# Four writes and one read for a turned tile, and a DRAM tile ordered by diagonal blocks

## The chip, the cores and the metric

The kernel runs on one core of one Trainium2 chip. The metric is the device time of one execution in microseconds (us), of which the median of several runs is taken. Before the change it is 2255.21 us (three runs, 2254.8 to 2257.08).

## The reference

One inference step of a two-layer hybrid recurrent decoder, for a prompt of 1024 tokens and for eight samples of one token each with states of their own, with the same float32 weights. The even layer has eight gated DeltaNet heads (GDN) beside eight mLSTM heads, the odd layer four GLA heads beside four retention heads:

```python
h = rms(x, norm_w) * (1.0 + scale) + shift
proj = h @ w_in                               # one projection per layer, 1024 -> several thousand columns
# GDN, per chunk of tokens:
A = where(tri_strict, decay * kk, 0.0) * beta
U = triangular_solve(A + eye, rhs, lower, unit_diagonal)
o = gam * (q @ S) + (qk * decay) @ U
S_new = exp(last) * S + k^T @ (exp(last - bh) * U)
# both branches:
y = concat(branch outputs) * silu(z)
x = x + gate * (y @ w_out)
```

What matters here is the triangular solve of GDN, and that keys and values are wanted both with channels and with tokens in the partitions, so that tiles have to be turned.

## The kernel before

All activations are kept with channels in the 128 partitions and 1032 columns (1024 prompt tokens, then eight samples). Prompt tokens are worked in eight chunks of 128. A projection to 128 channels is 72 matmuls of 344 columns into the three pj banks, with each weight tile split into a high and a low part (whi, wlo).

Nothing is issued in the order in which the Python stands. A `Recorder` takes down every operation with what it depends on (`add`, line 207, and `touch`, line 244), and `order` (line 274) plans all engines' queues with estimated durations: a list scheduler that runs forward, then backward for new priorities, up to ten times, and keeps the plan with the shortest estimated end. `emit` then issues the operations in that order, so that in the profile each carries the same line, 448. All DMAs go through one queue, SP. Each engine takes its instructions strictly in the planned order and waits at an instruction whose inputs aren't there, whatever stands behind it. The planner counts two accesses of a DRAM tile as dependent when their ranges from first to last element overlap (`region`, line 198), also where the elements themselves are interleaved and never the same. The built program's waits come from the tile framework and not from that rule.

Two helpers are touched by the change.

`squares` (line 1697) turns a tile: VectorE (DVE) transposes its 32 x 32 blocks into y, then the blocks are moved between partitions through a DRAM tile td (one of four, line 2145), and come back as z. Before, that is one DMA that writes y whole (512 KB) and four DMAs that read 32 partitions each (128 KB each). In one execution it is called 52 times. In the even layer there are 36: the keys and the values of each GDN head (written from s_kd and s_vs, by `gdn_mix`, line 1191), values and outputs of each mLSTM head (from s_va) and keys of each mLSTM pair (from s_kwe). In the odd layer there are 16, in `v_tokens` (line 1711). Tiles read back are named after the slot that they land in: s_N, s_v, s_mp, s_pt, s_qs, s_u.

`inverse` (line 1279), once for each GDN head, inverts eight 128 x 128 unit triangular matrices N. Their 32 x 32 diagonal blocks, four to a matrix (index j), are written to a DRAM tile nd by four DMAs of 32 KB, read back in one as 64 blocks of 16 x 16 in 64 partitions (into s_EM), inverted there in 15 steps of two DVE operations, written to a DRAM tile yd and read back by four DMAs. Small matmuls then build the whole inverse. (The tile yd of the inverse shares its name in the profile with the big tile yd that holds the mixer's output.) Before, rows of nd and yd are ordered by chunk c first, then j, then half q: the four writes interleave, and each one's range overlaps the next one's.

The 128 x 1024 tiles of weights are loaded into two slots wf0 and wf1, whose loads (wf<-in_ev_w_in, wf<-in_ada_w) wait for PE or DVE to free the slot, and stand in SP's queue among all else.

Of the kernel before, what the change touches and what calls it, by code (L numbers as in the profile page):

```python
# [9 lines left out]
F32 = mybir.dt.float32  # L10
# [7 lines left out]
T = 1024  # L18
# [6 lines left out]
NC = T // L  # L25
# [438 lines left out]
class Step:  # L464
# [814 lines left out]
    def inverse(self, N):  # L1279

        V, G, dma = self.nc.vector, self.nc.gpsimd, self.nc.sync.dma_start

        nd, yd = (self.nyd[x][self.turn(x, 2)] for x in ("nd", "yd"))
        by32 = lambda x, j: x.rearrange("(c j q) x -> c j (q x)", c=NC, j=4)[:, j, 0:1024].rearrange(
            "c (s t) -> s c t", t=32)
        by16 = lambda x: x[:, 0:512].rearrange("m (r t) -> m r t", t=32)[:, :, 0:16]
        blocks = [slice(32 * j, 32 * j + 32) for j in range(4)]
        t = self.slot("EM", name="inv")
        D, At, qt, Dt = (t[:, 256 * i:256 * i + 256].rearrange("p (c t) -> p c t", c=NC) for i in range(4))
        nb, yb, tb = (t[0:64, 256 * i:256 * i + 256].rearrange("p (r t) -> p r t", t=16) for i in (1, 2, 3))  # L1290
        dma(yb, self.a["i16"].rearrange("p (r t) -> p r t", t=16))
        for j, b in enumerate(blocks):
            dma(by32(nd, j), N[b, :, b])
        dma(nb, by16(nd))
        for s in range(15):
            n = 15 - s
            V.tensor_tensor(tb[:, 0:s + 1, 0:n], yb[:, 0:s + 1, s:s + 1].to_broadcast([64, s + 1, n]),
                            nb[:, s:s + 1, s + 1:16].to_broadcast([64, s + 1, n]), op=ALU.mult)
            V.tensor_tensor(yb[:, 0:s + 1, s + 1:16], yb[:, 0:s + 1, s + 1:16], tb[:, 0:s + 1, 0:n], op=ALU.subtract)
        dma(by16(yd), yb)  # L1300

        for j, b in enumerate(blocks):
            dma(D[b], by32(yd, j))
        V.transpose(Dt, D)
        p = self.ps(None, [128, NC, 32])
        for c in range(NC):
            for j, b in enumerate(blocks):
                self.mm(p[b, c, :], N[b, c, b], Dt[b, c, :], tile_position=(32 * j, 32 * j))
        V.tensor_tensor(At, p, self.imask.unsqueeze(1).to_broadcast([128, NC, 32]), op=ALU.mult)
        p = self.ps(None, [128, NC, 32])  # L1310
        for c in range(NC):
            for j, b in enumerate(blocks):
                self.mm(p[b, c, :], At[b, c, :], D[b, c, :], tile_position=(32 * j, 32 * j))
        V.tensor_tensor(D, D, p, op=ALU.subtract)
        V.transpose(Dt, D)
        Y = self.slot("Y", [128, NC, L], name="Y")
        G.memset(Y, 0.0)
        for b in blocks:
            V.tensor_copy(Y[b, :, b], D[b])

        p = self.ps(None, [128, 2, NC, 32])
        for c in range(NC):
            for i in (0, 2):
                j = i + 1
                bi, bj = slice(32 * i, 32 * i + 32), slice(32 * j, 32 * j + 32)
                self.mm(p[bj, 0, c, :], N[bi, c, bj], Dt[bi, c, :], tile_position=(32 * i, 32 * j))
        for j in (1, 3):
            bj = slice(32 * j, 32 * j + 32)
            self.act(qt[bj], p[bj, 0], AF.Copy, scale=-1.0)
        p2 = self.ps(None, [128, NC, 64])  # L1330
        for c in range(NC):
            for i in (0, 2):
                j = i + 1
                bi, bj = slice(32 * i, 32 * i + 32), slice(32 * j, 32 * j + 32)
                self.mm(p2[bi, c, 0:32], qt[bj, c, :], D[bj, c, :], tile_position=(32 * j, 32 * i))
            self.mm(p2[32:64, c, 0:32], D[32:64, c, :], qt[32:64, c, :], tile_position=(32, 32))
        V.tensor_copy(Y[0:32, :, 32:64], p2[0:32, :, 0:32])
        V.tensor_copy(Y[64:96, :, 96:128], p2[64:96, :, 0:32])

        iy = t[:, 0:512].rearrange("p (c t) -> p c t", c=NC)  # L1340
        Yt = iy[0:64]
        G.memset(Yt[0:32, :, 32:64], 0.0)
        G.tensor_copy(Yt[0:32, :, 0:32], Dt[0:32])
        G.tensor_copy(Yt[32:64, :, 32:64], Dt[32:64])
        V.tensor_copy(Yt[32:64, :, 0:32], p2[32:64, :, 0:32])
        p3 = self.ps(None, [128, NC, 64])
        for c in range(NC):
            self.mm(p3[64:128, c, :], N[0:64, c, 64:128], Yt[:, c, :], tile_position=(0, 64))
        q3 = iy
        self.act(q3[64:128], p3[64:128], AF.Copy, scale=-1.0)  # L1350
        p4 = self.ps(None, [128, NC, 64])
        for c in range(NC):
            self.mm(p4[0:64, c, :], q3[64:128, c, :], Y[64:128, c, 64:128], tile_position=(64, 0))
        V.tensor_copy(Y[0:64, :, 64:128], p4[0:64])
        return Y
# [341 lines left out]
    def squares(self, y, x, z):  # L1697


        dma = self.nc.sync.dma_start  # L1700
        y, z = y[:, 0:T], z[:, 0:T]
        self.nc.vector.transpose(y.rearrange("p (b c j) -> p b c j", b=4, c=NC),
                                 x[:, 0:T].rearrange("p (c b i) -> p b c i", b=4, c=NC))
        d = self.td[self.turn("td", 4)]
        dma(d, y)
        for b in range(4):
            dma(z[32 * b:32 * b + 32].rearrange("i (a x) -> i a x", a=4),
                d.rearrange("(a i) (b x) -> b i a x", a=4, b=4)[b])
        return z.rearrange("p (a c j) -> p c a j", a=4, c=NC)

    def v_tokens(self, v):
# [407 lines left out]
    def build(self):  # L2119
        tc, nc = self.tc, self.nc  # L2120
        with ExitStack() as ctx:
            cp = ctx.enter_context(tc.tile_pool(name="cp", bufs=1))
            psum = ctx.enter_context(tc.tile_pool(name="psum", bufs=1, space=PSUM))
            dr = ctx.enter_context(tc.tile_pool(name="dr", bufs=1, space=DRAM))
            self.big = {}
            for n in NAMES:
                for i in range(TAGS.get(n, 1)):
                    s = Slot(cp, f"s_{n}{i}", [128, SIZES.get(n, W)])
                    self.nc.slots[s.ap.name] = s
                    self.big[n, i] = s.ap  # L2130
            self.wt = {(n, i): cp.tile([128, 1024], F32 if n == "wf" else F32R, name=f"{n}{i}")
                       for n in WBUFS for i in range(WBUFS[n])}
            self.banks = {(n, i): psum.tile([128, 512], F32, name=f"{n}{i}")
                          for n in BANKS for i in range(BANKS[n])}
            self.arena = cp.tile([128, ARENA], F32, name="arena")
            self.base = cp.tile([128, BASE], F32, name="base")
            self.arena_at = {"base": 0, "even": 0, "odd": 0}
            self.xd = dr.tile([2, KT, 128, W], F32, name="xd")
            self.yd = dr.tile([16, 128, W], F32, name="yd")
            self.gd = dr.tile([4, 8, T], F32, name="gd")  # L2140
            self.ed = dr.tile([8, 8, 8], F32, name="ed")
            self.sd = [dr.tile([16, 128], F32, name=f"sd{i}") for i in range(2)]
            self.spd = dr.tile([16, W], F32, name="spd")
            self.rd = [dr.tile([4, QB], F32, name=f"rd{i}") for i in range(2)]
            self.td = [dr.tile([128, T], F32, name=f"td{i}") for i in range(4)]
            self.nyd = {x: [dr.tile([64, 528], F32, name=f"{x}{i}") for i in range(2)] for x in ("nd", "yd")}
            self.program()
            with tc.manual_schedule():
                self.nc.emit()
# [103 lines left out]
```

## Time and profile before

| what | value |
|---|---|
| median of three runs | 2255.21 us |
| profiled execution, its own time | 2262.98 us |
| its span, first to last instruction | 2261.2 us |
| mean granted TensorE clock | 0.983 |
| DMA traffic | 290.61 MB, mean 129 GB/s |

PE is TensorE's matmuls, PEld its weight loads, DVE VectorE, ACT ScalarE, POOL GpSimd, SP the queue that issues DMAs. A row of a stage gives the time span, then busy us and instruction count of each engine, the granted clock, the share of the DMA engines' time and GB/s. A row of waits gives an engine and the tile it writes, whom it waited for, us in total, times, longest. A row in order of time gives the start in us from the span's beginning, its us, engine, line, operation, output<-inputs, shapes and count; in brackets stands idle time just before and who ended it. On SP the time of a row is that of the issue, not of the transfer. The chain of work that ended last gives start, us and what.

### The profile page before, as it was taken

The page shows a single profiled execution, that of the slowest core. Times are in us where ns is not written, and L with a number is a line of the kernel's source. Part 1 is how long each engine was busy: PE and PEld are TensorE (multiplying, and loading weights), DVE is VectorE, ACT ScalarE, POOL GpSimd, SP SyncE. Part 2 cuts the span into 40 slices and gives each one's busy share as a digit, 9 for nine tenths or more (in the row PEclk, how much of TensorE's full clock was granted, in tenths as well). Part 3 has the DMA queues.
Part 4 walks back from the last instruction along what each step waited for, and adds up shares of the span by engine and source line. Part 5 has one row for each costly group of instructions (what it writes and reads, how often), then busy time and mean ns, then how long its engine had stood idle before and what let it go on. Part 6 is the DMA issues. An engine that isn't in the chain of part 4 may idle for free.

```text
span 2261.2 us, 42497 instructions
## 1 busy us (share of the span) xinstructions
PE 2184.1 (97%) x17532; PEld 2036.4 (90%) x17532; DVE 1312.8 (58%) x2559; ACT 761.4 (34%) x1374; POOL 588.4 (26%) x409
## 2 busy tenths in 40 slices
PE   6999999999999998998989999999999999999998
PEld 4877877999999988998889999999999999999997
DVE  6775656576565756666553355745754754755322
ACT  4432313242323323232341135234335334334322
POOL 3120212121121311202330032623622622634210
PEclk9999989999999999999999999999999999999999
DMA  9465564625172535527383222254253253365212
GB/s 263 134 190 161 138 190 115 177 78 149 48 189 75 160 99 123 137 77 189 100 253 117 74 80 69 73 153 124 76 157 119 76 162 106 110 192 176 81 59 92
DMA packets 323383, 290.61 MB, mean 129 GB/s; under 512 B 51963, under 2 KB 289013, under 8 KB 323182
## 3 DMA queue, kind: packets, MB, share of 16 engines
q1 hardware_dynamic: 323190, 287.91, 45.2%
q8 instruction: 137, 2.24, 0.4%
q14 instruction: 56, 0.46, 0.1%
HBM read 213.61 MB, written 74.44 MB: 127 GB/s over the span
## 4 chain that ended last, share of the span: by engine, by line
PE 81%; DMA 8%; DVE 6%; ACT 2%; issue 2%; SPq 1%; POOL 0%; POOLq 0%; ACTq 0%; DVEq 0%
PE pj L448 63%; PE A L448 12%; PE B L448 5%; SPq L448 1%; DMA wf<-in_ada_w 1%; DMA s_mp<-td 1%; DVE s_pt L448 1%; DVE wlo L448 1%; DMA s_h<-in_x_prompt 1%; DVE s_tmp L448 1%; DVE arena L448 1%; DMA td<-s_va 1%; DMA s_pt<-yd 0%; DMA td<-s_vs 0%; DMA s_pt<-td 0%
## 5 line engine op out<-in xcount | busy, mean ns | idle before, releaser
L448 PE MATMUL pj<-s_h,whi 128*128 128x344 f32 (+1 forms) x6024 | 1500.0, 328 | 3.7 <-DVE s_h L448 2.6
L448 PEld LDWEIGHTS pj<-s_h,whi 128*128 128x128 f32 (+1 forms) x6024 | 1046.5, 190 | 33.2 <-issue 19.8
L448 PE MATMUL pj<-s_h,wlo 128*128 128x344 f32 (+1 forms) x3024 | 985.2, 326 | 1.0 <-POOL s_h L448 0.6
L448 PEld LDWEIGHTS pj<-s_h,wlo 128*128 128x128 f32 (+1 forms) x3024 | 573.2, 190 | 12.1 <-issue 8.2
L448 ACT ACTIVATE whi<-wf 128x1024 fp32r<-128x1024 f32 (+1 forms) x146 | 152.1, 1042 | 355.1 <-PE pj L448 309.4
L448 DVE TENSOR_TENSOR wlo<-wf,whi 128x1024 fp32r<-128x1024 f32 x112 | 153.3, 1369 | 195.5 <-ACT whi L448 190.9
L448 ACT ACTIVATE s_pt<-pj 128x344 f32<-128x344 f32 (+1 forms) x170 | 76.7, 452 | 237.0 <-PE pj L448 232.4
L448 POOL TENSOR_TENSOR arena<-arena,base 128x8 f32<-128x8 f32 (+5 forms) x38 | 62.2, 1638 | 286.2 <-DVE arena L448 286.2
L448 POOL TENSOR_TENSOR wlo<-wf,whi 128x1024 fp32r<-128x1024 f32 (+1 forms) x32 | 77.4, 2419 | 169.0 <-ACT whi L448 163.5
L448 POOL TENSOR_TENSOR s_tmp<-s_EM 128x512 f32<-128x512 f32 (+1 forms) x60 | 81.3, 1368 | 81.7 <-DVE s_N L448 28.5
L448 DVE SCALAR_TENSOR_TENSOR s_pt<-s_u,base,s_pt 128x1024 f32<-128x1024 f32 x72 | 95.3, 1323 | 0.1
L448 ACT ACTIVATE s_u<-pj 128x344 f32<-128x344 f32 x93 | 41.2, 452 | 136.6 <-PE pj L448 86.8
L448 DVE SCALAR_TENSOR_TENSOR arena<-arena,A 128x128 f32<-128x128 f32 (+1 forms) x84 | 32.8, 390 | 92.5 <-PE A L448 92.4
L448 DVE SCALAR_TENSOR_TENSOR s_zz<-s_pt,pj 128x344 f32<-128x344 f32 x96 | 48.7, 507 | 62.8 <-ACT s_pt L448 62.1
L448 POOL TENSOR_TENSOR s_tmp<-s_tmp,arena 128x1024 f32<-128x1024 f32 (+2 forms) x26 | 45.3, 1747 | 83.2 <-PE B L448 34.2
L448 POOL MEMSET s_u<- 128x3 f32 x24 | 2.5, 102 | 243.4 <-DVE s_pt L448 243.4
L448 POOL TENSOR_TENSOR s_kd<-s_kd,s_vs 128x1032 f32<-128x1032 f32 x8 | 20.0, 2506 | 169.2 <-ACT s_vs L448 169.2
L448 ACT ACTIVATE s_tmp<-s_tmp 128x1024 f32<-128x1024 f32 (+1 forms) x44 | 46.1, 1057 | 35.7 <-POOL s_tmp L448 34.1
L448 DVE TENSOR_TENSOR s_EM<-s_EM 64x15 f32<-64x15 f32 (+7 forms) x240 | 49.9, 208 | 14.2 <-DMA s_EM<-nd 9.0
L448 DVE SCALAR_TENSOR_TENSOR arena<-arena,B 64x130 f32<-64x130 f32 (+1 forms) x84 | 31.2, 372 | 44.4 <-PE B L448 43.6
L448 ACT ACTIVATE arena<-A,arena 128x128 f32<-128x128 f32 x64 | 23.5, 367 | 92.9 <-PE A L448 92.7
L448 ACT ACT_TABLE_LOAD x41 | 52.6, 1283 | 5.1 <-DMA s_h<-in_x_prompt 4.3
(639 smaller groups left out, 3550.4 us busy)
## 6 DMA issues: line engine op xcount, KB each, us to landing
wf<-in_ev_w_in SPq DMA_DIRECT2D x64, 512.0 KB
wf<-in_od_w_in SPq DMA_DIRECT2D x48, 512.0 KB
wf<-in_ada_w SPq DMA_DIRECT2D x32, 512.0 KB
s_tmp<-sd SPq DMA_DIRECT2D x24, 512.0 KB
s_pt<-yd SPq DMA_DIRECT2D x16, 516.0 KB
td<-s_kd SPq DMA_DIRECT2D x16, 512.0 KB
td<-s_vs SPq DMA_DIRECT2D x16, 512.0 KB
s_v<-td SPq DMA_DIRECT2D x64, 128.0 KB
```

The costliest lines, as they stand in the source:

```text
L448: op.fn(*[self.placed(x) for x in op.args], **{k: self.placed(x) for k, x in op.kw.items()})
```

## The change

In `squares`, the write is cut into four DMAs, one for each 32 partitions a of y; each writes one quarter d[a] of the DRAM tile, whose shape becomes [4, 128, 256], in rows of 1 KB. One DMA reads the whole of it back into z. In `inverse`, rows of nd and yd are ordered by diagonal block j first, then chunk c, then half q, so that each of the four writes fills a range of its own. The 16 x 16 inversion works on whichever block lies in a partition, so nothing else changes with it.

```diff
-        by32 = lambda x, j: x.rearrange("(c j q) x -> c j (q x)", c=NC, j=4)[:, j, 0:1024].rearrange(
+        by32 = lambda x, j: x.rearrange("(j c q) x -> j c (q x)", c=NC, j=4)[j, :, 0:1024].rearrange(
             "c (s t) -> s c t", t=32)
...
         d = self.td[self.turn("td", 4)]
-        dma(d, y)
-        for b in range(4):
-            dma(z[32 * b:32 * b + 32].rearrange("i (a x) -> i a x", a=4),
-                d.rearrange("(a i) (b x) -> b i a x", a=4, b=4)[b])
+        for a in range(4):
+            dma(d[a].rearrange("(b i) x -> i b x", b=4), y[32 * a:32 * a + 32].rearrange("i (b x) -> i b x", b=4))
+        dma(z.rearrange("p (a x) -> p a x", a=4), d.rearrange("a p x -> p a x"))
...
-            self.td = [dr.tile([128, T], F32, name=f"td{i}") for i in range(4)]
+            self.td = [dr.tile([4, 128, 256], F32, name=f"td{i}") for i in range(4)]
```

Since the planner sees other dependencies and other sizes, it makes another order for the whole program. SP issues 990 DMAs before and after, and PE has the same matmuls.

On SP, at the inverse of the second GDN head, before (s_N0 is N, s_v20 the turned values of GDN, s_mp0 a turned mLSTM tile; in brackets the semaphores waited for, DMAHW those of DMAs):

```order
L448 DMA nd1_134<-s_N0_70 32x8x32 [waits DMAHW6_49]
L448 DMA wf1_105<-in_ev_w_in 128x8x128 [waits DMAHW7_49,PE_49]
L448 DMA s_v20_65<-td1_130 32x4x256 [waits DMAHW3_49,DMAHW0_49]
L448 DMA s_v20_65<-td1_130 32x4x256 [waits DMAHW1_49]
L448 DMA wf0_104<-in_ada_w 128x1024 [waits DMAHW2_49,DVE_49]
L448 DMA s_v20_65<-td1_130 32x4x256
L448 DMA s_v20_65<-td1_130 32x4x256 [waits DMAHW4_49]
L448 DMA nd1_134<-s_N0_70 32x8x32 [waits DMAHW5_49]
```

The same place now:

```order
L448 DMA nd1_134<-s_N0_70 32x8x32 [waits DMAHW3_49,DVE_49]
L448 DMA nd1_134<-s_N0_70 32x8x32 [waits DMAHW4_49]
L448 DMA nd1_134<-s_N0_70 32x8x32
L448 DMA nd1_134<-s_N0_70 32x8x32 [waits DMAHW6_49]
L448 DMA wf1_105<-in_ev_w_in 128x8x128 [waits DMAHW0_49,PE_49]
L448 DMA s_EM0_69<-nd1_134 64x16x16 [waits DMAHW5_49,DMAHW6_49,DMAHW4_49,DMAHW3_49]
```

Before, the third and the fourth write have a turned tile's four reads and two weight loads between them. Now the four stand together, and one weight load is between them and the read of the whole. That the four are adjacent holds in all eight heads.

On SP, a turned mLSTM tile near the second head, now (td2 is the DRAM tile, s_va0 what is written):

```order
L448 DMA td2_131<-s_va0_75 32x4x256 [waits DMAHW7_49,DVE_49]
L448 DMA td2_131<-s_va0_75 32x4x256 x2
L448 DMA wf0_104<-in_ada_w 128x1024 [waits DMAHW5_49,DMAHW2_49,PE_49]
L448 DMA td2_131<-s_va0_75 32x4x256 [waits DMAHW3_49]
L448 DMA s_mp0_78<-td2_131 128x4x256 [waits DMAHW3_49,DMAHW1_49,DMAHW4_49,DMAHW0_49,DMAHW7_49,Activation_49,Pool_49]
```

Before, the like place had its four reads in a row, behind the landing of a single write. Now a weight load that waits for PE stands between the third and the fourth write, and the read of the whole comes behind that.

## The prediction

> **What bounds the kernel now.** I read the page's head first, then the busy times by stage, then the waits of PE (TensorE's matmul row), then the time-ordered view of the queues around the two steps that change. The page's head:
>
> ```profile
> span 2261.2 us, 42497 instructions
> PE 2184.1 (97%) x17532; PEld 2036.4 (90%) x17532; DVE 1312.8 (58%) x2559; ACT 761.4 (34%) x1374; POOL 588.4 (26%) x409
> DMA  9465564625172535527383222254253253365212
> ```
>
> PE is busy for 97% of the span, every other engine for less than two thirds, and the DMA engines are rarely full. The change takes no matmul away. So it can only move PE's idle time, 2261.2 - 2184.1 = 77 us in all. Where that lies, by stage (setup, even layer, the rest; behind the times stand the busy times and counts of PE, PEld, DVE, ACT and POOL, the granted clock, the DMA share and GB/s):
>
> ```profile
> 0.00:100.00 100.00, 80.73 (x639) 65.05 (x640) 68.08 (x148) 47.89 (x97) 31.14 (x47) 0.95 0.71 204
> 100.00:1200.00 1100.00, 1056.56 (x8436) 963.35 (x8435) 692.21 (x1542) 333.07 (x663) 223.71 (x167) 0.98 0.52 140
> 1200.00:2261.00 1061.00, 1046.83 (x8461) 1008.01 (x8460) 552.47 (x870) 380.48 (x615) 333.60 (x195) 0.99 0.37 109
> ```
>
> The inverse runs in the even layer alone, and there PE is idle for 1100 - 1056.56 = 43.4 us. After it, 14.2 us are left, and only 16 of the 52 turned tiles, so what the change does to the odd layer I cost at nothing. Who ended PE's idle time between 100 and 1200 us:
>
> ```profile
> PE pj L448 <- DMA wf<-in_ada_w: 10.3, 3, 4.3
> PE A L448 <- DVE arena L448: 8.7, 1, 8.7
> PE B L448 <- ACT s_va L448: 6.0, 2, 5.5
> PE B L448 <- DVE arena L448: 4.3, 4, 2.8
> PE A L448 <- DVE s_tmp L448: 3.7, 2, 1.9
> PE pj L448 <- ACT s_mq L448: 3.5, 1, 3.5
> PE A L448 <- DVE s_EM L448: 0.2, 1, 0.2
> ```
>
> The tile in which the inverse is worked, s_EM, ended 0.2 us of PE's idle time. PE does not wait at the inverse: it projects the next head meanwhile. The long waits are single events. The longest, and what stood ahead of it, first on SP (the queue that issues all DMAs), then on DVE, then on PE:
>
> ```profile
> 882.58 0.38 SPq L448 DMA_DIRECT2D td<-s_va  x1
> 886.24 9.03 SPq L448 DMA_DIRECT2D s_mp<-td  x4
> ```
> ```profile
> 902.42 0.48 DVE L448 SCALAR_TENSOR_TENSOR s_zz<-s_mp,base,s_zz 128x256 f32<-128x256 f32 x1 [10.16 <-DMA s_mp<-td]
> ```
> ```profile
> 905.06 0.38 PE L448 MATMUL A<-base,arena 128*8 128x128 f32 x1 [8.71 <-DVE arena L448]
> ```
>
> This is a turned tile: written at 882.58, read back in four pieces from 886.24, of whose issue SP spent 9.03 us. DVE stood behind it in its own order, and PE behind DVE, with the next projection planned right behind. An engine's order is fixed when the program is built; a step that is late against the plan holds all that is planned behind it. That is how a DMA off PE's path costs PE 8.7 us. One more wait of PE has a turned tile ahead of it (a piece of the chain that ended last, and PE's row; ACT copies s_pt to s_va between them):
>
> ```profile
> 1062.26 4.41 DMA s_pt<-td
> ```
> ```profile
> 1068.05 0.77 PE L448 MATMUL B<-s_va,s_kwe 128*128 128x130 f32 x2 [5.50 <-ACT s_va L448]
> ```
>
> **The inverse's four writes.** They are nd<-s_N; the read of the whole is s_EM<-nd. First head, fourth head, eighth head:
>
> ```profile
> 163.94 0.80 SPq L448 DMA_DIRECT2D nd<-s_N  x2
> 169.06 0.31 SPq L448 DMA_DIRECT2D nd<-s_N  x1
> 172.31 0.43 SPq L448 DMA_DIRECT2D nd<-s_N  x1
> 178.34 0.64 SPq L448 DMA_DIRECT2D s_EM<-nd  x1
> ...
> 514.80 1.82 SPq L448 DMA_DIRECT2D nd<-s_N  x4
> 526.10 0.63 SPq L448 DMA_DIRECT2D s_EM<-nd  x1
> ...
> 1028.03 0.53 SPq L448 DMA_DIRECT2D nd<-s_N  x1
> 1040.04 1.74 SPq L448 DMA_DIRECT2D s_v<-td  x4
> 1044.11 0.45 SPq L448 DMA_DIRECT2D nd<-s_N  x1
> 1050.48 0.65 SPq L448 DMA_DIRECT2D s_EM<-nd  x1
> ```
>
> In the fourth head the four are issued in 1.82 us, so the chip does not hold one until another has landed; only the planner believes that they overlap, spaces them, and fills the room with other DMAs. In the eighth head a turned tile's reads stand between, which wait in their turn. First write to read takes 178.34 - 163.94 = 14.4, 11.3 and 22.45 us in these three; the mean of all eight, from the first of these rows to the last, is 17.5. With the writes apart, the built order has the four together in all eight heads. I price that at 1.8 us of issue and 6.0 us from last write to read (172.31 to 178.34), 7.8 us; the fourth head gives the worse bound, 11.3. The saving is 17.5 - 7.8 = 9.7 us a head, 78 us over eight, at least 50 by the other bound.
>
> Nearly all of it is off the path: PE waited 0.2 us there. What it can do is indirect: the inverse comes sooner behind its matmuls and less stands in SP's queue between waits. I credit it by the named waits: of the three for wf (10.3 us; weight loads that stand behind other waits on SP) about one, 3.4 us; and of the tail behind the eighth head (s_tmp and s_mq, 7.2 us) about a third, 2.4 us. That is -5.8, rounded to **-6 us**. Bounds: 0 (all hidden), and -20 (about half of the 43.4 us).
>
> **The turned tiles.** 52 of them pass through DRAM. Each was one write of 512 KB and four reads of 128 KB; now it is four writes and one read. Five issues either way, the same bytes. The pieces of the round trip have these rows, from the chain that ended last (a 512 KB write, and the last of four reads) and from SP:
>
> ```profile
> 882.58 3.64 DMA td<-s_va
> 1122.60 3.18 DMA s_pt<-td
> ```
> ```profile
> 1120.25 2.78 SPq L448 DMA_DIRECT2D s_pt<-td  x4
> ```
>
> Before, undisturbed: 3.64 for the write, three issues at about 0.45 (1.35, by the pace of the 1.82 us for four), 3.18 for the last read: 8.2 us. Now: 1.35 of issue, 3.18 for the last write if a piece written costs what a piece read does, 3.64 for the read in one: 8.2 us. Term 0. The rows in DRAM are now written in 1 KB runs where they were 4 KB; no row here prices that, so I allow 1.5 us a tile either way, nearly all beside PE's projections. If the cover is gone, a late tile costs PE what the one above did, 8.7 us.
>
> The Trainium skill ("DMA: Bandwidth & Descriptors", Rules for kernel authors) says to coalesce many small transfers into one large one, which speaks against the split writes as much as for the single read. The trace has four reads issued from 1120.25 with the last landed at 1122.60 + 3.18 = 1125.78, 5.5 us for all four, far from four full trips (12.7): pieces overlap, so I take 0 and not a loss.
>
> Order inside a set is new, though. In 9 of the 52 sets the planner puts other issues between the four writes, in four of them weight loads that wait for PE (one such place is shown with the change); before, a write could not be torn, and 5 sets of reads were. Against this, issues that stand anywhere inside a set fall from 161 to 138. I call it even. The whole list is reordered besides, so single stalls like that at 905.06 are dealt anew; that is the range, about one such stall either way.
>
> **Sum.** The profiled execution took 2262.98 us, its span 2261.2 and 1.8 around it. 2261.2 - 6 + 1.8 = 2257.0 on that scale. It stands 7.8 us over the median of the timed runs, 2255.21, so there the forecast is **2249.2 us**, 0.27% faster. About 0.2%, 4.5 us, is what a measurement of this kernel can tell from no change.
>
> **Rivals.**
> *Nothing changes.* PE's matmuls are the same, and 0.2 us was waited for at the inverse; the 9.7 us a head are hidden by projections. For it: the 97%. Against it: 43.4 us of idle time that a reordering hardly leaves as it was. Time 2255. Chance 0.24.
> *Slower: a torn write.* The single read needs the last of four pieces; where a weight load that waits for PE stands ahead of that piece in SP's queue, the read and its users come late, and DVE and PE behind them as at 905.06. Place: the first two heads, where most of the torn even-layer sets lie. It decides once the last piece is issued over 3.64 us behind the first, since then the whole write of before would have landed. Price 8.7 us for one such event net of those removed: 2264. Chance 0.21.
> *Slower: pieces one after another.* If a coalesced transfer were what the DMA engines need, four writes would take 4 x 3.18 = 12.7 us for 3.64, 9.1 us more on each of the 36 tiles in the even layer; two of them reached PE before (8.7 and 5.5 us), so two more would, 14.2 us: about 2269. [...] Against it stands the 5.5 us for four. Chance 0.05.
> *Much faster.* The inverse does pace the even layer: its chain ends sooner, the scan behind it too, and half of the 43.4 us is filled: 2255 - 20 = 2235. Against it: the 0.2 us. Chance 0.12.
> The forecast itself, 2241 to 2250.7: 0.38.
>
> **Chances and range.** Faster by over 0.2% is the forecast and the last rival, 0.38 + 0.12 = 0.50; within 0.2% is 0.24; slower 0.21 + 0.05 = 0.26. Both signs are likely, so the forecast's own range, 2241 to 2250.7, stands beside the whole. The range for 8 in 10 runs from near the much-faster case, 2236, to one stall more, 2264; it leaves out the worst of both ends.
>
> **What would show it.** Right: first write to read of nd at 6 to 11 us in all eight heads; PE's busy time within 5 us of 2184; PE's idle time between 100 and 1200 us at 35 to 40; td from first write to last landing about 8 us where nothing stands between. Wrong: PE idle there over 50 with a wait whose chain leads to a td set whose writes lie far apart (torn write); writes of one set landing more than 10 us after the first though issued together (serial pieces); idle under 25 (the inverse paced it); or a shift of the same size in the setup or in the odd layer, which would say that the new order as a whole did it and neither edit.

## The result and the profile after

| | before | after |
|---|---|---|
| median of five runs each, us | 2256.29 (2254.8 to 2258.27) | 2243.84 (2238.14 to 2246.91) |
| ratio, 95% interval | | 0.9942 [0.9925, 0.9958] |
| profiled execution, us | 2262.98 | 2242.51 |
| its span, us | 2261.2 | 2240.7 |
| its PE busy time, us | 2184.1 | 2174.0 |
| its PE idle time, us | 77.1 | 66.7 |
| its mean granted clock | 0.983 | 0.989 |

By the medians the change makes the kernel 12.45 us faster, 0.55%; the ratio of the runs puts it at 0.58%. The forecast was 6 us. The two profiled executions are further apart, 20.5 us, because the one of before lies 6.7 us over its median and the one of after 1.3 under. Half of these 20.5 us is PE's idle time (10.4), the other half PE's busy time (10.1), at the same 17532 matmuls.

The head of the page of after:

```profile
span 2240.7 us, 42464 instructions
PE 2174.0 (97%) x17532; PEld 2027.2 (90%) x17532; DVE 1307.6 (58%) x2559; ACT 762.3 (34%) x1374; POOL 586.7 (26%) x409
```

The same stages of after (busy us and counts of PE, PEld, DVE, ACT and POOL, then the granted clock, the DMA share and GB/s):

```profile
0.00:100.00 100.00, 80.68 (x645) 64.71 (x645) 69.25 (x149) 48.66 (x98) 31.11 (x47) 0.95 0.70 201
100.00:1200.00 1100.00, 1070.46 (x8566) 979.34 (x8566) 702.52 (x1562) 336.74 (x669) 224.93 (x167) 0.99 0.51 143
1200.00:2240.00 1040.00, 1022.88 (x8325) 983.18 (x8323) 535.83 (x849) 376.89 (x607) 330.68 (x195) 1.00 0.36 109
```

Setup has the same idle time as before (19.3 us) and the part behind 1200 us 17.1 where it had 14.2. The gain is all in the even layer: 29.5 us idle where there were 43.4, and 8566 matmuls done in the stretch that held 8436. The shift does not grow after that: PE's first matmul pj<-s_va,whi of the even layer's output projection starts at 1197.06 us where it started at 1218.60, 21.5 us earlier, and the span ends 20.5 us earlier.

PE's waits in that stretch of after (us in total, times, longest):

```profile
PE B L448 <- DVE arena L448: 4.1, 6, 1.7
PE A L448 <- DVE s_q L448: 3.8, 1, 3.8
PE A L448 <- issue: 3.0, 3, 2.1
PE pj L448 <- ACT s_qs L448: 2.9, 1, 2.9
PE A L448 <- DVE s_tmp L448: 2.6, 1, 2.6
PE A L448 <- DVE s_EM L448: 2.3, 1, 2.3
...
PE B L448 <- ACT s_va L448: 0.8, 1, 0.8
PE A L448 <- DVE arena L448: 0.7, 1, 0.7
...
PE pj L448 <- DMA wf<-in_ada_w: 0.3, 1, 0.3
```

The three groups with the long waits of before are nearly gone: wf from 10.3 us to 0.3, arena into A from 8.7 to 0.7, s_va from 6.0 to 0.8. The longest single wait is 3.8 us instead of 8.7. New waits, on s_q and s_qs, stand in part of their place.

The inverse's writes and the read of the whole, in time on SP, for the first, fourth and eighth head of after:

```profile
159.89 1.91 SPq L448 DMA_DIRECT2D nd<-s_N  x4
...
166.53 0.63 SPq L448 DMA_DIRECT2D s_EM<-nd  x1
...
505.07 1.02 SPq L448 DMA_DIRECT2D td<-s_vs  x2
506.14 3.02 SPq L448 DMA_DIRECT2D nd<-s_N  x4
511.61 2.45 SPq L448 DMA_DIRECT2D td<-s_vs  x2
...
515.32 0.64 SPq L448 DMA_DIRECT2D s_EM<-nd  x1
516.05 1.46 SPq L448 DMA_DIRECT2D s_v<-td  x1
...
1011.87 1.82 SPq L448 DMA_DIRECT2D nd<-s_N  x4
...
1020.40 0.64 SPq L448 DMA_DIRECT2D s_EM<-nd  x1
```

The four writes stand together, and the first write is 6.64, 9.17 and 8.53 us ahead of the read; over the eight heads the mean is 6.1, where it was 17.5. So this went as foreseen. Whether it is what made the kernel faster is for the experiments. The fourth head also shows a torn turned tile: the last two writes of td follow 6.5 us behind the first two. So does the first head, where the first write of the values stands at 126.81 us and the other three from 133.50 on.

### The profile page after: what moved, and what is told of

Same layout as the page of the kernel before. It is cut to its first block, busy times and chain, and to the rows that moved or that the text cites. A ratio compares the mean times of both kernels' runs of the same rounds, so it can differ in the third digit from the quotient of the medians.

```text
span 2240.7 us, 42464 instructions
## 1 busy us (share of the span) xinstructions
PE 2174.0 (97%) x17532; PEld 2027.2 (90%) x17532; DVE 1307.6 (58%) x2559; ACT 762.3 (34%) x1374; POOL 586.7 (26%) x409
## 4 chain that ended last, share of the span: by engine, by line
PE 80%; DVE 8%; DMA 7%; issue 2%; POOL 1%; ACT 1%; SPq 1%; POOLq 0%; DVEq 0%; ACTq 0%
PE pj L448 63%; PE A L448 12%; PE B L448 4%; DMA s_tmp<-sd 1%; SPq L448 1%; DVE arena L448 1%; DVE s_pt L448 1%; DVE s_tmp L448 1%; DMA s_tmp<-in_state_gla 1%; DVE s_N L448 1%; POOL s_qg L448 1%; DVE s_zz L448 1%; DVE wlo L448 1%; DVE s_h L448 1%; DMA s_Y<-rd 1%
## 5 line engine op out<-in xcount | busy, mean ns | idle before, releaser
L448 DVE TENSOR_TENSOR wlo<-wf,whi 128x1024 fp32r<-128x1024 f32 x112 | 146.4, 1307 | 220.5 <-ACT whi L448 217.2
L448 DVE SCALAR_TENSOR_TENSOR s_pt<-s_u,base,s_pt 128x1024 f32<-128x1024 f32 x72 | 100.4, 1395 | 0.3
```

Source lines behind the costliest of these rows:

```text
L448: op.fn(*[self.placed(x) for x in op.args], **{k: self.placed(x) for k, x in op.kw.items()})
```

## The experiments

Four theories were put against each other; the expectations name them by letters. **A**: the planner's false order among the four writes of nd was the cost, and the new layout takes it away. **B**, later **D**: any new order of the queues deals the single stalls anew, and this one fell well; the edits do nothing by themselves. **C**, later **E**: the new transfers of the turned tiles are the gain. **F**: with the new transfers the planner's picture fits the chip better, so that its orders are better on the whole. Each kernel was timed in five rounds against the kernel before on the same chip: the first four kernels on one chip, the next four on another, the last four on a third.

### Each edit alone

In the first, the kernel before gets the new order of nd's rows and nothing else; in the second, the kernel after gets the old one back.

```diff
 # e1_nd_alone, from before
-        by32 = lambda x, j: x.rearrange("(c j q) x -> c j (q x)", c=NC, j=4)[:, j, 0:1024].rearrange(
+        by32 = lambda x, j: x.rearrange("(j c q) x -> j c (q x)", c=NC, j=4)[j, :, 0:1024].rearrange(
 # e2_td_alone, from after: the same two lines, the other way
```

> The kernel before with the edit to the inverse's DRAM tile alone. Theory A (the planner's false order among the four writes was the cost): most of the 12.4 us, so 2244 to 2249, with first write to read of nd at 4 to 9 us in all eight heads. Theory B (a new order by luck): anywhere from 2240 to 2262, with no relation to nd. Theory C (the turned tiles made the gain): 2254 to 2258.

> The change without the edit to the inverse's tile: turned tiles written in four and read in one. Theory A: 2253 to 2258, since the turned tile's round trip has the same sum, and nd stays at some 17 us. Theory B: anywhere from 2240 to 2262. Theory C: 2244 to 2249.

Measured: nd alone 1.0020 [1.0008, 1.0033], turned tiles alone 0.9913 [0.9898, 0.9927]. (The times in the expectations are on the scale of the result, where before took 2256.29 us; on this chip it took 2248.72.) The stage of the even layer and PE's waits in it, of the kernel with nd alone:

```profile
100.00:1200.00 1100.00, 1054.63 (x8481) 964.61 (x8481) 697.62 (x1557) 333.82 (x667) 225.47 (x167) 0.98 0.52 142
```
```profile
PE pj L448 <- DMA wf<-in_ada_w: 8.9, 3, 7.5
PE B L448 <- issue: 8.0, 1, 8.0
PE pj L448 <- ACT whi L448: 5.7, 1, 5.7
```

and of the kernel with the turned tiles alone, with nd's writes and read in its fourth head:

```profile
100.00:1200.00 1100.00, 1074.51 (x8663) 985.50 (x8663) 705.74 (x1571) 339.15 (x672) 231.72 (x167) 0.99 0.51 144
```
```profile
PE B L448 <- DVE arena L448: 5.6, 7, 2.3
PE pj L448 <- ACT s_u L448: 4.3, 1, 4.3
...
PE pj L448 <- DMA wf<-in_ada_w: 0.8, 2, 0.5
```
```profile
507.64 0.33 SPq L448 DMA_DIRECT2D nd<-s_N  x1
...
510.04 0.57 SPq L448 DMA_DIRECT2D nd<-s_N  x1
510.92 1.84 SPq L448 DMA_DIRECT2D td<-s_vs  x4
512.80 0.45 SPq L448 DMA_DIRECT2D nd<-s_N  x1
...
517.07 0.49 SPq L448 DMA_DIRECT2D nd<-s_N  x1
...
521.17 0.63 SPq L448 DMA_DIRECT2D s_EM<-nd  x1
```

With nd alone, first write to read is 3.1 to 10.4 us over the eight heads (mean 5.5), shorter than in after, and the kernel is no faster: PE is idle 45.4 us, with a wf wait of 7.5 us and two other waits of 8.0 and 5.7. With the turned tiles alone, nd takes 8.1 to 16.2 us and its writes stand apart again, and the kernel gains at least as much as with both edits (0.9913 against 0.9942, measured on different chips, the intervals just touching): PE is idle 25.5 us and wf ends 0.8 us of it. The waits for wf do not follow nd. Theory A falls. Both results would also fit theory C, that the turned tiles made the gain; exchanging the transfers, further down, tests that.

### The order without the layout

Here the kernel before keeps its layout in DRAM, and only the planner is told that the four writes do not overlap. The planned order is then that of e1_nd_alone (in the traces every engine runs the same sequence in both); the addresses in DRAM differ.

```diff
 # e3_planner_told, from before, in region
-            hi = ap.offset + sum(s * (n - 1) for s, n in dims) + 1
-            return 0, 1, ap.offset, hi
+            j = ap.offset // 1056 if [list(x) for x in dims] == [[32, 32], [4224, 8], [1, 32]] else -1
+            return (0, 4, ap.offset, ap.offset + sum(s * (n - 1) for s, n in dims) + 1) if j < 0 else (j, j + 1, 0, 33792)
```

> The kernel before, DRAM layout and all, but the planner is told that the four writes of nd don't touch each other. Every engine's instructions and waits then stand as in the kernel with the nd edit alone; only the addresses in DRAM differ. Theory A: the same time as that kernel within 0.1%, since the layout does nothing on the chip. Rival (the layout itself matters, four ranges apart being faster to write): slower than that kernel by 2 us or more, near 2256.

Measured: 1.0022 [1.0005, 1.0039], against 1.0020 with the layout. The layout in DRAM does nothing by itself, and the order that it gives costs 0.2%. The profiled executions of these two, 2247.9 and 2257.0 us of span, show how far one execution lies from another of the same order.

### The order dealt anew, without either edit

Two estimates of the planner are changed by 4 and by 2 ns. Nothing else in the kernel is touched, but the order of all queues comes out differently.

```diff
 # e4_before_redealt, from before
-    DRAIN = 170.0
+    DRAIN = 174.0
 # e7_before_redealt_2, from before; e8_after_redealt, from after
-    OVERLAP = dict(vector=80.0, scalar=98.0, gpsimd=42.0)
+    OVERLAP = dict(vector=78.0, scalar=98.0, gpsimd=42.0)
```

> A control: the kernel before with one estimate of the planner moved by 4 ns (its DRAIN from 170 to 174 ns), so that another order comes out with neither edit. Theory A: within 4 us of 2256, as nd is still spaced out. Theory B: as far from 2256 as the change is, 8 to 15 us, to either side.

> A second control: the kernel before with another estimate moved by 2 ns (OVERLAP of DVE from 80 to 78 ns), another order with neither edit. Theory D: away from the kernel before by 0.2% to 1% to either side. If orders of this kernel differ little and the 0.9959 of the first control was an outlier: within 0.2%.

> The changed kernel with the same estimate moved by 2 ns. Theory D: anywhere from 0.985 to 1.003 of the kernel before. Theory E: 0.990 to 0.997, as the transfers are the same as in the changed kernel.

Measured: 0.9959 [0.9944, 0.9974] and 0.9958 [0.9941, 0.9975] from before, and 0.9899 [0.9879, 0.9919] from after, the lowest ratio of the study (2229.72 us where before took 2252.60 on that chip). A change of 2 to 4 ns in one estimate, with none of the change under study, gives about 70% of its gain, twice. Theory B has what it needs: a new order alone can move this kernel by most of the effect.

### The order and the transfers exchanged

To part the transfers from the order, each plan is kept as it is and the DMAs in it are replaced. In the first kernel all engines have the planned order of before; at the old write's place four writes of 1 KB rows are issued, at the first old read's place one read, and nothing at the other three. The second has the order of after, with one write at the first piece's place and four reads at the single read's.

```diff
 # e5_old_order_new_tiles, from before, at the end of squares
+        e, ops, nothing = self.td2[(self.at["td"] - 1) % 4], self.nc.ops[-5:], lambda: None
+        real = ops[0].fn
...
+        ops[0].fn, ops[0].args = write, (e, y)     # four DMAs into [4, 128, 256]
+        ops[1].fn, ops[1].args = read, (z, e)      # one DMA
+        for o in ops[2:]:
+            o.fn, o.args = nothing, ()
 # e6_new_order_old_tiles, from after, at the same place
+        ops[0].args = (e, y)                       # one DMA into [128, T]
+        ops[4].fn, ops[4].args = read, (z, e)      # four DMAs
+        for o in ops[1:4]:
+            o.fn, o.args = nothing, ()
```

> The order planned for the kernel before, on all engines, but each turned tile written in four pieces (where its one write stood) and read in one (where the first of its four reads stood). Theory D (the order dealt by the planner makes the time, the transfers nothing): within 3 us of the kernel before. Theory E (the new transfers are themselves quicker, or free SP sooner): faster by 8 us or more.

> The order planned for the changed kernel, on all engines, but each turned tile written in one (where its first piece stood) and read in four (where its one read stood). Theory D: as fast as the changed kernel, a ratio to the kernel before of 0.990 to 0.996. Theory E: the gain goes, a ratio of 0.998 or more.

Measured: 0.9991 [0.9975, 1.0007] and 0.9981 [0.9967, 0.9995]. The new transfers in the old order are worth nothing that can be measured, so theory E falls as it was put: whatever they save, by themselves they do not make the kernel faster. The new order with the old transfers gains 0.2%, where after gained 0.6%. Here theory D missed (it said 0.990 to 0.996) and theory E's figure, 0.998 or more, came out. The intervals of e6 and after are apart, though on different chips, so the order's gain seems to hang in part on the transfers that it was planned for. The even layer of e6, and its waits for wf:

```profile
100.00:1200.00 1100.00, 1069.10 (x8523) 978.19 (x8522) 698.96 (x1558) 334.77 (x666) 223.96 (x167) 0.98 0.51 142
```
```profile
PE pj L448 <- DMA wf<-in_ada_w: 1.2, 2, 1.0
```

PE's idle time there, 30.9 us, is near the 29.5 of after, and the waits for wf are gone as in after. So the new order takes these stalls away with either form of the transfer. Why the whole kernel then gains less is not shown; its profile loses more to a low clock in the even layer, 20.9 us against 13.5, summed as below, but that is one execution of each.

The first of the two, e5, shows where a stall belongs. Its waits of PE in the even layer, the row of the longest, SP ahead of it, the landing of the read (from the chain that ended last) and DVE's wait for it:

```profile
PE pj L448 <- DMA wf<-in_ada_w: 9.6, 2, 5.4
PE A L448 <- DVE arena L448: 7.1, 1, 7.1
```
```profile
895.48 0.37 PE L448 MATMUL A<-base,arena 128*8 128x128 f32 x1 [7.07 <-DVE arena L448]
```
```profile
879.24 0.46 SPq L1717 DMA_DIRECT2D s_mp<-td  x1
880.08 7.16 SPq L448 DMA_DIRECT2D s_EM<-in_i  x1
```
```profile
879.24 13.58 DMA s_mp<-td
```
```profile
892.84 0.48 DVE L448 SCALAR_TENSOR_TENSOR s_zz<-s_mp,base,s_zz 128x256 f32<-128x256 f32 x1 [8.53 <-DMA s_mp<-td]
```

The same matmul waits 7.07 us where it waited 8.71 before, and the same wf waits are back, with other transfers of the turned tile. Before, SP's 9.03 us at this place were at the four reads of td. Here the read is one DMA, issued in 0.46 us, and SP is held for 7.16 us at the next one, a load that has nothing to do with turned tiles. The read itself lands only 13.58 us after its issue, and DVE waits 8.53 us for it, as it waited 10.16 us before. So this stall belongs to the place in the order and not to the form of the transfer. The wait for s_va, 6.0 us before, does not come back: it is 1.1 us in e5.

### A better picture of the chip, or a worse one

If the new form were faster because the planner judges it more rightly, then its estimates should carry the gain over. By the expectations, the reads of td land later than planned before, and closer to the plan in the new form, by about 1.7 us a set; no row here shows the plan's own times. In the first two kernels the planner is told so, by that much, in one direction for before and in the other for after. The other two are these with the order dealt anew.

```diff
 # e9_before_planner_later_reads, from before (e10_after_planner_sooner_read, from after: -1700.0)
+        op.cost += 1700.0 * (queue == "sync" and reads[0].name.startswith("td"))
...
-            return 450.0 + op.size / op.rate + (2100.0 if op.size > 1 << 18 else 1400.0)
+            return 450.0 + op.size / op.rate + (2100.0 if op.size > 1 << 18 else 1400.0) + op.cost
...
-                end = dma + (2100.0 if op.size > 1 << 18 else 1400.0)
+                end = dma + (2100.0 if op.size > 1 << 18 else 1400.0) + op.cost
 # e11_before_later_reads_redealt and e12_after_sooner_read_redealt: besides
+    OVERLAP = dict(vector=78.0, scalar=98.0, gpsimd=42.0)
```

> The kernel before, transfers as they were, but the planner is told that every read of a turned tile lands 1.7 us later than it reckoned. (In the trace of before these reads land later than planned; in the new form the plan fits better. 1.7 us is about the difference a set.) Theory F (the new form's gain is that its plan fits the chip better): 0.990 to 0.995 of the kernel before, as with the new tiles. Theory D (orders differ by luck): 0.995 to 1.003, as the four orders with old tiles so far.

> The changed kernel, but the planner is told that the single read lands 1.7 us sooner than it reckoned, so that its plan is as hopeful as that for the old tiles. Theory F: the gain goes, 0.996 to 1.002 of the kernel before. Theory D: any order's value; if orders with new tiles are simply better, 0.989 to 0.995.

> As the kernel before with its planner told of later reads, and the DVE estimate moved by 2 ns for another order. Theory F: 0.990 to 0.995. Theory D: 0.995 to 1.003.

> As the changed kernel with its planner told of a sooner read, and the DVE estimate moved by 2 ns for another order. Theory F: 0.996 to 1.002. Theory D, if orders with new tiles are simply better: 0.989 to 0.995.

Measured, in this order: 0.9993 [0.9978, 1.0007], 1.0021 [1.0005, 1.0037], 1.0003 [0.9989, 1.0017], 0.9940 [0.9919, 0.9960]. The better estimate brings before nothing, in either deal. The worse one takes the whole gain from after in one deal and leaves it in the other. Theory F falls as far as this estimate goes; a program with both edits can be 0.2% slower than before or 0.6% faster by one number in the planner.

### What the twelve say together

| orders planned with | ratios to before | mean | spread (standard deviation) |
|---|---|---|---|
| the new turned tiles | 0.9942, 0.9913, 0.9899, 1.0021, 0.9940 | 0.9943 | 0.0047 |
| the old ones | 1, 1.0020, 0.9959, 0.9958, 0.9993, 1.0003 | 0.9989 | 0.0025 |

(1 is the kernel before itself; e3 has e1's order and counts once; e5 and e6 have transfers that were not planned for and are left out.) The means differ by 0.0046, the standard error of that is 0.0023: sqrt(0.0047²/5 + 0.0025²/6). Two standard errors from so few orders, on several chips, settle nothing; and four of the five ratios with the new tiles rest on 4 to 6 executions, where most others rest on 12. Shown is that orders of one and the same program lie far apart: with both edits between 0.9899 and 1.0021, with the old tiles between 0.9958 and 1.0020. That the new form is better on the average stays open.

The kernels e2 and e8, 0.9913 and 0.9899, lie below after, 0.9942; of the two, only e8's interval is apart from after's, and both were timed on other chips.

## Why the prediction was right, and where it was not

**The forecast's sign** was right, and so was its own range, 2241 to 2250.7, in which 2243.84 lies; but not for its reason, so that is luck. The -6 us were credited to the inverse's four writes; with those alone the kernel is 0.2% slower. The prediction's last sentence on what would show it wrong named what happened, the new order as a whole, but looked for it in the setup or in the odd layer. It came in the even layer, where it looked like the edits' doing.

**The inverse's writes: "first write to read of nd at 6 to 11 us in all eight heads".** They took 3.9 to 9.2 us, four of them under 6, mean 6.1 where 7.8 was worked out. Some 91 us of latency (8 x 11.4) were saved where 78 were worked out, and with nd alone none of it reached the end of the kernel. The step that failed is the next one, "I credit it by the named waits": one wf wait and a third of the tail. The wf waits lost 10.0 us, three times the 3.4 credited, but they do so without the nd edit too (0.8 us in e2) and stay with it alone (8.9 us in e1). Of the 7.2 us of s_tmp and s_mq called the tail, 5.4 lie behind 1000 us; they are gone in after, and in e1 too, where one wait of 8.0 us stands behind 1000 us instead. The row of before that said 0.2 us was waited for at s_EM was the better evidence, and it was set aside.

**The turned tiles: "Term 0".** Right in the order of before: 0.9991 for the transfers alone. In the new order, e6 leaves it open. In the even layers of the two traces, as far as landings can be told from the semaphores, a 512 KB write landed after 5.0 us on the mean and a piece of the new write after 3.7, a piece read after 4.6 and the whole read after 4.6. Sets whose four writes stand together had all landed 4.9 us after the first issue on the mean, so the pieces overlap as the prediction took it. The 1.5 us a tile that were allowed for 1 KB rows were not needed.

**"Single stalls like that at 905.06 are dealt anew; that is the range, about one such stall either way".** This is where the experiments point, and it was used for the range alone: the new transfers gain nothing in the old order (e5), the new layout of nd nothing by itself (e1 against e3), and new orders without either edit up to 0.4% (e4, e7). How much of the 0.6% the order gives without the new transfers is open (0.2% in e6). The price of one stall was too low as well. The 5 us windows of before at the stall (columns as in the stages, the granted clock third from the end):

```profile
900.00:905.00 5.00, 0.00 (x0) 0.00 (x0) 2.49 (x10) 0.04 (x1) 0.00 (x0) 0.51 0.07 15
905.00:910.00 5.00, 4.94 (x18) 4.94 (x19) 3.28 (x10) 2.43 (x3) 0.00 (x0) 0.50 0.55 166
910.00:915.00 5.00, 5.00 (x33) 5.00 (x32) 1.23 (x3) 0.46 (x1) 2.40 (x2) 0.97 0.97 235
```

While PE waits the clock falls to half, and it stays there for the next 5 us, in which 18 matmuls are done where the next window does 33. So this stall cost 8.7 us of idle time and, by an estimate from these rows, some 2.5 (4.94 x 0.5) of busy time. The Trainium skill ("TensorE: Matmul & The Clock Gate", Part 1) says that the clock is gated to half behind an idle window of about 3.4 us and returns after about as long a busy one. The 0.50 in these rows agrees; the return, from 910 us on, comes some 5 us after PE starts again at 905.06.

**"PE's busy time within 5 us of 2184".** Wrong: 2174.0. This step failed outright: the prediction took the change to move only PE's idle time, since the matmuls are the same, and put any change of its busy time at nothing. In windows of 5 us, the busy time times what the clock lacks to 1 sums to 26.2 us before and 17.0 after, of that 19.5 and 13.5 in the even layer. The idle time in the even layer fell by 13.9 us and this loss by 6.0: together 19.9 of the 20.5 us between the two profiles. Part of the clock's share may belong to these two executions and not to the order: the profile of before has a mean clock of 0.983, the low end of what before shows on another chip (last section). "PE's idle time between 100 and 1200 us at 35 to 40" came out at 29.5, since more of the stalls went than were credited.

**The rivals.** *Nothing changes* was right on what the layout and the transfers are worth in an unchanged order (e1 against e3, and e5) and wrong on the order. *A torn write* did occur, in the first and the fourth head: the late writes are over 6 us behind the first, well over the 3.64 from which it was to decide. In the fourth head no wait of PE was over 2.3 us; in the first the longest was 3.8, and its chain leads to another transfer (s_N<-ed), not to td. So neither decided. *Pieces one after another* falls with e5: written in pieces in the same order, nothing is lost. The Trainium skill's rule on coalescing ("DMA: Bandwidth & Descriptors", Rules for kernel authors), which had been cited against the split writes, calls a transfer under 64 KB mostly overhead. At 128 KB a piece against 512 KB this case shows no cost. *The inverse paces the even layer* falls with e1, where the inverse comes as soon as in after and the kernel is no faster.

## What to carry to other kernels

Where a planner fixes the order of in-order queues, an edit that it sees deals the whole order anew. With TensorE busy 97% of the time, a new order alone moved the kernel without the edits to between 0.4% faster and 0.2% slower, and the kernel with them to between 1.0% faster and 0.2% slower: time an edit in several orders (change an estimate by a few ns) before its gain is called its own, and keep the best order found. To part an edit from its order, keep the plan and exchange what is issued at its places. A stall of TensorE is priced with what the clock loses behind it, and a shorter latency of a step for which TensorE hardly waited is priced at nothing.

## What the runs showed of the hardware

**The clock also halves behind waits of 1.6 and 2.1 us, among small matmuls.** At the eighth head of after, where the inverse's small matmuls run with few others between:

```profile
1045.00:1050.00 5.00, 5.00 (x153) 4.55 (x152) 1.95 (x6) 0.16 (x1) 0.00 (x0) 1.00 0.92 219
1050.00:1055.00 5.00, 2.90 (x73) 2.43 (x75) 1.77 (x7) 0.75 (x2) 0.72 (x2) 0.80 0.01 4
1055.00:1060.00 5.00, 5.00 (x51) 4.45 (x45) 2.15 (x5) 1.28 (x8) 0.39 (x1) 0.50 0.01 2
1060.00:1065.00 5.00, 5.00 (x31) 4.65 (x31) 1.02 (x2) 1.33 (x2) 1.64 (x1) 0.50 0.01 3
```
```profile
1052.49 0.63 PE L448 MATMUL A<-s_EM,s_N 32*32 32x32 f32 x27 [2.10 <-issue]
```

The longest wait is 2.1 us, and the clock is at 0.50 for the two windows that follow, in which PE counts as busy throughout. In e10 it is at half from 545 to 560 us, with PE counted as busy for all of it; the last wait ahead is one of 1.6 us, ended at 543.00 by small matmuls:

```profile
545.00:550.00 5.00, 5.00 (x66) 4.21 (x55) 2.87 (x8) 2.24 (x10) 0.85 (x2) 0.50 0.66 179
550.00:555.00 5.00, 5.00 (x69) 4.41 (x69) 1.59 (x4) 0.00 (x0) 0.39 (x1) 0.50 0.02 5
555.00:560.00 5.00, 5.00 (x32) 4.53 (x32) 1.02 (x2) 0.59 (x1) 0.00 (x0) 0.50 0.00 0
```

Why is not settled; the ends of matmuls, and so the busy time shown, are modelled.

**The granted clock differs from execution to execution of one program.** The kernel before took 2246.08 to 2265.28 us in 29 executions on one chip, at mean clocks of 0.983 to 0.989; the longer ones have the lower clock (correlation -0.72, and -0.68 and -0.48 on the two other chips). That is wider than the whole effect of the change, so its size rests on medians, and a single pair of profiles, as 20.5 us here against 12.45, overstates it. The median of before itself was 2256.29 us on the chip of the result and 2248.72, 2252.60 and 2249.03 on the three of the experiments; the change as a whole was timed on the first alone.

**One DMA issue can hold SP for over 7 us** (7.54 of the 9.03 us before, at the second of the four reads; 7.16 in e5, at another DMA in the same place). In the windows of 5 us in which the holds begin, the DMA engines moved only 78 GB/s (885 to 890 us before) and 21 GB/s (880 to 885 in e5), where the mean of the kernel before is 129. What held the issue was not tried.
